# A two-layer hybrid decoder trunk on one core: low-rank products, merged steps, GpSimd's norm work and the expert stage's gathers rearranged

## The chip, the cores and the metric

The kernel runs on one core of one Trainium2 chip. The metric is the device time of one execution in microseconds (us). The kernel before takes 1657.32 us (median of three runs, 1655.43 to 1660.0). In the text TensorE is the matrix engine (PE in the rows, its weight loads PEld), VectorE is DVE, ScalarE is ACT, GpSimd is POOL, and SyncE (SP) issues the DMA transfers. Every instruction queue works in its own program order, and engines wait for each other by semaphores.

## The reference

256 tokens of width 1024 go through two layers. Each layer is a mixer and an expert stage, each followed by a layer norm of `ALPHA * h + result`:

```python
for l in range(DEPTH):                                   # 2
    z = h @ w_in[l]                                      # gates, conv, RWKV-7, attention
    y_a = (conv_b * causal_depthwise_conv(conv_c * conv_h, conv_w)) @ p_a
    y_b = rwkv7_time_mix(...) @ p_b                      # decay = f(tanh(xw) @ w2), a = sigmoid(a0 + xa @ a2)
    y_c = dilated_attention_branch(z_attn, cos, sin) @ p_c
    mix = (gate_a * y_a + gate_b * y_b + gate_c * y_c) @ w_o
    h = layer_norm(ALPHA * h + mix, ln1_g[l], ln1_b[l])
    # group-limited top-2 of 16 experts, SwiGLU
    for e in range(16):
        hid = silu(h @ w_gate[e]) * (h @ w_up[e])        # 1024 -> 512
        ffn += combine[..., e:e + 1] * (hid @ w_down[e]) # 512 -> 1024
    h = layer_norm(ALPHA * h + ffn, ln2_g[l], ln2_b[l])
```

All of it is float32.

## The kernel before, in words

**Dense products.** A float32 operand is split into a rounded high part and the rounded remainder (`hilo`: ScalarE casts, VectorE or GpSimd subtracts), and a product is three matmuls (`mm3`, lines 400 to 402). Names ending in h and l are such parts (wh, wl of a weight tile, xh, xl of the tokens), `dw` and `dt` are the dense products' PSUM banks. A matmul of rounded parts (fp32r) is one pass; one of plain float32 is two passes, and the trace has a record for each. Weight tiles of 512 KB are loaded ahead (`AHEAD` = 5 tiles) and split ahead (`SPLIT` = 2).

**Mixer.** A written table (`STAGES`) sets the order of the dense stages: waves (four per layer: r, k, v of four RWKV heads each), convolutions, attention heads, gates and output products. What belongs to a stage beside the dense product is a chain, a generator (`lows`, `wave`, `attention`). After every four steps of a dense product `pump` lets each live chain go on to its next `yield`; TensorE's queue thus holds dense matmuls with short groups of a chain's matmuls between them. The groups that matter here: in `wave` the low-rank products `pw` (decay) and `pa` (a), lines 490 to 495, whose high parts have 128 rows and whose remainder products 64, and the products `zb` (line 616, four pairs on alternating row halves, with a `yield` after two of them); in `attention` the scores `sc` (line 893, with a `yield` between two pairs of heads).

**Norm of the mixer's input.** The tokens that feed the dense products are transposed and split first (`xc`, `xh`, `xl`). The gain and offset for the residual copy of h (`ng`, `nb`) are loaded, GpSimd multiplies and adds (lines 1078, 1079: four operations of 128x1024), and SyncE stores the result to `hsave` (line 1080), from where it is read back at the mixer's end. This stands ahead of the first wave.

**Expert stage.** Tokens are ranked per expert, 64 places for each. Experts go in pairs p = 0 to 7, with shared work for each two pairs (even p). `places` (line 1303) makes the 0/1 matrix O of a group of four experts on VectorE. `gather` (line 1336) makes their tokens xg by matmul with O: in plain float32 from h, or, once `us` is set (at p = 4), from its rounded parts uh and ul. `gu` are the gate and up products (line 1389), `ht` the transposed hidden rows, `db` the down products (line 1440), `back` (line 1371) adds the weighted rows with the transposed O (`OT`) to the accumulators `acc`. `rows` (lines 1354 to 1364) makes OT by four transposes and the places' weights cs by four matmuls with two columns. At p = 7 the residual is added by float32 matmuls with ALPHA times the identity (line 1427), after GpSimd has applied gain and offset to h at p = 6. The expert weights (192 loads of 512 KB per layer, tiles `raw` and `mo`) are float32 and go straight into matmuls. After the last pair all engines read a count and may branch to an overflow path, which is not taken here.

Of the kernel before, what the change touches and what calls it, by code (L numbers as in the profile page):

```python
# [20 lines left out]
NE = 16  # L21
# [18 lines left out]
def _constants():  # L40
# [22 lines left out]
    out["alpha"] = ALPHA * np.eye(128)  # L63
# [163 lines left out]
class Net:  # L227
# [238 lines left out]
    def wave(self, l, w, r, k, v, lo, low, vf, yb):  # L466
# [21 lines left out]
        ps = self.bank("pw")  # L488
        for j in range(2):
            nc.tensor.matmul(ps[:, j * 256:j * 256 + 256], lh[:, 0, j * 128:j * 128 + 128], xh[:, 0, :], start=True, stop=False)  # L490
            nc.tensor.matmul(ps[:, j * 256:j * 256 + 256], lh[0:64, 0, j * 128:j * 128 + 128], xl[0:64], start=False, stop=True)
        pa = self.bank("pa")
        for j in range(2):
            nc.tensor.matmul(pa[:, j * 256:j * 256 + 256], lh[:, 1, j * 128:j * 128 + 128], xh[:, 1, :], start=True, stop=False)
            nc.tensor.matmul(pa[:, j * 256:j * 256 + 256], lh[64:128, 1, j * 128:j * 128 + 128], xl[64:128], start=False, stop=True)
# [365 lines left out]
    def attention(self, l, hh, g, q, k, v, st, yc):  # L861
# [24 lines left out]
        for qb in range(2):  # L886
# [3 lines left out]
            for hp in range(2):  # L890
# [3 lines left out]
                if hp == 0:  # L894
                    yield
# [98 lines left out]
    def mixer(self, l, h, vf):  # L994
# [238 lines left out]
    def moe(self, l, u, r, nm, lg):  # L1233
# [90 lines left out]
        V.tensor_copy(cnti, cnt)  # L1324
        over = s16("over")
# [20 lines left out]
        def rows(O, p):  # L1346

            b = self.bank("ot")
            ot = self.tg([128, 2, 256], "OT", F32R)
            cb = self.bank("cs")  # L1350
            for pp in range(2):
                for i in range(2):
                    o = O[:, i, 2 * pp:2 * pp + 2, :].rearrange("p e t -> p (e t)").bitcast(F32)
                    nc.tensor.transpose(b[:, pp * 256 + i * 128:pp * 256 + i * 128 + 128], o, self.c("ident"))
                for i in range(2):
                    o = O[:, i, 2 * pp:2 * pp + 2, :].rearrange("p e t -> p (e t)").bitcast(F32)
                    e = 2 * p + 2 * pp
                    nc.tensor.matmul(cb[:, 2 * pp:2 * pp + 2], o, comb[:, i, e:e + 2], start=(i == 0), stop=(i == 1))  # L1358
            V.tensor_copy(ot.rearrange("p a b -> p (a b)"), b)
            cs = self.sm([128, 2], "cs")  # L1360
            cv = cb[:, 0:4].rearrange("p (a e) -> p a e", e=2)
# [3 lines left out]
            return ot, cs  # L1365
# [13 lines left out]
        for p in range(NE // 2):  # L1379
            gu = []  # L1380
            for what in range(2):
                b = self.bank("gu")
                for k in range(KC):
                    if k % 2 == 0:
                        raw = [self.next_raw() for _ in range(2)]
                        if p == 0 and what == 0 and k + AH < KC:
                            gather(nxt, xg, k + AH)
                    for e in range(2):
# [3 lines left out]
                if what == 0:  # L1392
                    if late is not None:
                        back(*late)
                    if p % 2 == 0:
                        ot, cs = rows(nxt, p)
                        if p + 2 < NE // 2:
                            nxt, xn = places(p // 2 + 1), self.pair([128, 4, 2, 128], "xg")
                    if p == 4:

                        us = (self.pair([128, D], "uh", F32R), self.pair([128, D], "ul", F32R))
# [196 lines left out]
```

## Time and profile before

| | |
|---|---|
| median of three runs | 1657.32 us |
| profiled execution, its span | 1654.77 us, 1653.0 us |
| TensorE busy, mean granted clock | 1598.7 us (97%), 0.989 |
| VectorE, ScalarE, GpSimd busy | 956.6, 688.8, 75.8 us |
| moved by DMA | 370.02 MB, mean 224 GB/s |

A timeline row gives the start in us from the start of the span, the duration, engine, line, operation, names (written <- read), shape and count; a row with a count stands for that many instructions from its start on. In brackets is the idle time before it and who ended it. Matmul durations overlap, so the time that one takes in a stream is read from one start to the next. A layer of the mixer takes some 560 us, the expert stage some 235: layer 0 is mixer to 576 and expert stage from 586 to 822, layer 1 starts its dense work at 836.

### The profile page before, as it was taken

To read this page: it belongs to the slowest core of one execution; us is meant where nothing else is said; L and a number is where in the kernel's file an instruction comes from. 1 tells how busy PE (TensorE), PEld (TensorE's weight loads), DVE (VectorE), ACT (ScalarE), POOL (GpSimd) and SP (SyncE) were. 2 spreads that over 40 slices of the span, in tenths; PEclk is the share of its full clock that TensorE was granted. 3 is DMA by queue.
4 is the path that set the end of the run, shared out by engine and by line. 5 is a ranking of instruction groups with operands and counts; after the bars stand their busy time and mean duration, and the time that the engine had idled before them with its cause. 6 is when DMAs were issued, how large, how long until landed. Compare 5 with 4: busy or idle time off the path is not lost. (4 is left out here: it accounts for less than half of the span.)

```text
span 1653.0 us, 38103 instructions
## 1 busy us (share of the span) xinstructions
PE 1598.7 (97%) x16296; PEld 1254.0 (76%) x16296; DVE 956.6 (58%) x1768; ACT 688.8 (42%) x1236; POOL 75.8 (5%) x96
## 2 busy tenths in 40 slices
PE   6999999999999999999989999999999999999996
PEld 6999998988999954433379998899889999444332
DVE  6777767968765631121278678778687656211213
ACT  4554766757443311111145456666765433101110
POOL 4000000000000000002120000000000000000020
PEclk9999999999999999999989999999999999999998
DMA  8544443333458979999744434434334489799992
GB/s 308 174 133 153 136 140 97 129 116 100 141 169 304 355 294 405 409 409 383 274 167 138 147 123 129 132 122 129 120 109 155 154 333 359 290 410 410 409 402 86
DMA packets 102704, 370.02 MB, mean 224 GB/s; under 512 B 11392, under 2 KB 12416, under 8 KB 102528
## 3 DMA queue, kind: packets, MB, share of 16 engines
q1 hardware_dynamic: 102528, 367.51, 61.3%
q8 instruction: 130, 2.13, 0.5%
q14 instruction: 46, 0.38, 0.1%
HBM read 363.27 MB, written 4.19 MB: 222 GB/s over the span
## 5 line engine op out<-in xcount | busy, mean ns | idle before, releaser
L400 PE MATMUL dw<-xh,wh 128*128 128x256 f32 (+1 forms) x1584 | 472.6, 299 | 3.3 <-ACT wh L324 2.3
L401 PE MATMUL dw<-xl,wh 128*128 128x256 f32 (+1 forms) x1584 | 450.2, 284 | 5.7 <-DVE xl L325 5.7
L402 PE MATMUL dw<-xh,wl 128*128 128x256 f32 (+1 forms) x1584 | 449.6, 284 | 2.1 <-DVE wl L325 2.1
L325 DVE TENSOR_TENSOR wl<-raw,wh 128x1024 fp32r<-128x1024 f32 x272 | 329.6, 1224 | 55.3 <-ACT wh L324 24.6
L400 PEld LDWEIGHTS dw<-xh,wh 128*128 128x128 f32 (+1 forms) x1584 | 302.1, 191 | 25.1 <-issue 8.2
L324 ACT CAST wh<-raw 128x1024 fp32r<-128x1024 f32 x278 | 284.1, 1044 | 67.5 <-DVE wl L325 44.7
L401 PEld LDWEIGHTS dw<-xl,wh 128*128 128x128 f32 (+1 forms) x1584 | 303.2, 191 | 8.4 <-DVE xl L325 7.4
L402 PEld LDWEIGHTS dw<-xh,wl 128*128 128x128 f32 (+1 forms) x1584 | 302.9, 191 | 3.1 <-DVE wl L325 2.8
L1389 PE MATMUL gu<-raw,xg 128*64 128x512 f32 x592 | 139.0, 599 | 1.9 <-PE cs L1358 1.9
L1445 DVE SCALAR_TENSOR_TENSOR yl<-db,cs,yh 128x512 fp32r<-128x512 f32 x32 | 24.0, 751 | 148.0 <-ACT yh L1444 148.0
L1389 PEld LDWEIGHTS gu<-raw,xg 128*64 128x64 f32 x592 | 45.2, 137 | 81.1 <-issue 74.7
L1389 PE MATMUL gu<-mo,xg 128*64 128x512 f32 x432 | 104.0, 599 | 0.0
L1440 PE MATMUL db<-raw,hT 128*64 128x512 f32 x352 | 82.4, 596 | 1.3 <-ACT hT L1421 1.3
L1389 PEld LDWEIGHTS gu<-mo,xg 128*64 128x64 f32 x432 | 31.6, 138 | 55.5 <-issue 55.2
L1444 ACT ACTIVATE yh<-db,cs 128x512 fp32r<-128x512 f32 x32 | 22.0, 688 | 116.7 <-PE db L1440 116.7
L1410 ACT ACTIVATE th<-gu 128x512 f32<-128x512 f32 x16 | 9.6, 598 | 136.8 <-PE gu L1389 136.8
L1421 ACT COPY hT<-ht 128x512 f32<-128x512 f32 x16 | 9.4, 586 | 136.4 <-PE ht L1419 136.4
L1440 PEld LDWEIGHTS db<-raw,hT 128*64 128x64 f32 x352 | 25.1, 137 | 50.9 <-issue 47.9
L1412 DVE TENSOR_TENSOR th<-th,gu 128x512 f32<-128x512 f32 x16 | 11.0, 688 | 87.8 <-PE gu L1389 87.8
L400 PE MATMUL dt<-wh,xh 128*128 128x256 f32 x192 | 57.9, 302 | 0.0
L1411 DVE SCALAR_TENSOR_TENSOR th<-th,gu 128x512 f32<-128x512 f32 x16 | 11.0, 688 | 80.5 <-ACT th L1410 80.4
L401 PE MATMUL dt<-wl,xh 128*128 128x256 f32 x192 | 54.7, 285 | 0.0
(368 smaller groups left out, 2858.9 us busy)
## 6 DMA issues: line engine op xcount, KB each, us to landing
raw<-in_wm SPq DMA_DIRECT2D x272, 512.0 KB, 3.6
raw<-in_we SPq DMA_DIRECT2D x236, 512.0 KB, 10.2
mo<-in_we SPq DMA_DIRECT2D x148, 512.0 KB, 10.2
lo<-in_lo SPq DMA_DIRECT2D x8, 512.0 KB, 3.6
ng<-in_norms SPq DMA_DIRECT2D x5, 512.0 KB, 10.2
nb<-in_norms SPq DMA_DIRECT2D x5, 512.0 KB, 10.2
raw<-in_wl SPq DMA_DIRECT2D x4, 512.0 KB, 8.4
hsave<-h SPq DMA_DIRECT2D x4, 512.0 KB, 2.8
```

The costliest lines, as they stand in the source:

```text
L324: r = self.nc.scalar.copy(hi, src)
L325: (eng or self.nc.vector).tensor_tensor(lo, src, hi.bitcast(F32), op=ALU.subtract)
L400: nc.tensor.matmul(out, lh, rh, start=first, stop=False)
L401: nc.tensor.matmul(out, lh, rl, start=False, stop=False)
L402: nc.tensor.matmul(out, ll, rh, start=False, stop=last)
L1389: nc.tensor.matmul(b[64 * e:64 * e + 64, :], xg[k // 4][:, k % 4, p % 2, 64 * e:64 * e + 64], raw[e][:, k % 2, :], start=(k == 0), stop=(k ...
L1410: nc.scalar.activation(t, gu[0], AF.Tanh, scale=0.5)
L1411: V.scalar_tensor_tensor(t, t, 1.0, gu[0], op0=ALU.add, op1=ALU.mult)
L1412: V.tensor_tensor(t, t, gu[1], op=ALU.mult)
L1440: nc.tensor.matmul(b[64 * e:64 * e + 64, :], ht[:, k, 64 * e:64 * e + 64], raw[e][:, k % 2, :], start=(k == 0), stop=(k == 3))
L1444: last = nc.scalar.activation(yh, b, AF.Copy, scale=w)
L1445: V.scalar_tensor_tensor(yl, b, w, yh.bitcast(F32), op0=ALU.mult, op1=ALU.subtract)
```

## The change

Nine edits. In `wave` the four 128-row matmuls of `pw` and `pa` stand first, then the four 64-row ones, changing between the two row halves and banks. The `yield` inside the `zb` groups and the one inside the `sc` groups are gone. GpSimd's four operations and hsave are written after the first stage of the mixer (n == 1). In the expert stage a constant tile `pick` holds the identity and both halves' combine weights in rounded parts; `rows` uses two matmuls of 160 columns per spot (transposed O and weights in one), in two spots: after the first product and in the middle of the second, and the next `places` follows the second spot. The split into uh and ul is made at p = 0 after its own gathers, on ScalarE and VectorE. The residual is written to the same uh and ul, scaled by ALPHA and split again at p = 7, and added with the identity in rounded parts. The constant `alpha` is gone.

```diff
@@ wave
-        for j in range(2):
-            nc.tensor.matmul(ps[...], lh[:, 0, ...], xh[:, 0, :], start=True, stop=False)
-            nc.tensor.matmul(ps[...], lh[0:64, 0, ...], xl[0:64], start=False, stop=True)
-        pa = self.bank("pa")
-        for j in range(2):
-            nc.tensor.matmul(pa[...], lh[:, 1, ...], xh[:, 1, :], start=True, stop=False)
-            nc.tensor.matmul(pa[...], lh[64:128, 1, ...], xl[64:128], start=False, stop=True)
+        for n, b in enumerate((ps, pa)):
+            for j in range(2):
+                nc.tensor.matmul(b[...], lh[:, n, ...], xh[:, n, :], start=(j == 0), stop=False, ...)
+        for j in range(2):
+            for n, b in enumerate((ps, pa)):
+                o = slice(64 * n, 64 * n + 64)
+                nc.tensor.matmul(b[...], lh[o, n, ...], xl[o], start=False, stop=True, ...)
@@ wave, zb
-                if c == 1:
-                    yield
@@ attention, sc
-                if hp == 0:
-                    yield
@@ mixer
-        g, b = self.norm_params(2 * l)
-        for i in range(2):
-            nc.gpsimd.tensor_tensor(h[i], h[i], g, op=ALU.mult)
-            nc.gpsimd.tensor_tensor(h[i], h[i], b, op=ALU.add)
-            nc.sync.dma_start(self.hsave[l, i], h[i])
...
         for n, (what, j) in enumerate(STAGES[l]):
+            if n == 1:
+                g, b = self.norm_params(2 * l)
+                for i in range(2):
+                    nc.gpsimd.tensor_tensor(h[i], h[i], g, op=ALU.mult)
+                    nc.gpsimd.tensor_tensor(h[i], h[i], b, op=ALU.add)
+                    nc.sync.dma_start(self.hsave[l, i], h[i])
@@ expert stage
+        for i in range(2):
+            wh, wl = (pick[...] for j in range(2))
+            self.hilo(wh, wl, comb[:, i, :])
-        def rows(O, p):
+        def rows(O, p, pp, ot, cs):
+            n = 2 * NE
             b = self.bank("ot")
-                    nc.tensor.transpose(b[...], o, self.c("ident"))
...
-                    nc.tensor.matmul(cb[:, 2 * pp:2 * pp + 2], o, comb[:, i, e:e + 2], start=(i == 0), stop=(i == 1))
-            V.tensor_copy(ot.rearrange("p a b -> p (a b)"), b)
+            for i in range(2):
+                o = O[:, i, 2 * pp:2 * pp + 2, :].rearrange("p e t -> p (e t)")
+                nc.tensor.matmul(b[:, 128 * i:128 * i + 128 + n], o, pick[:, n * (1 - i):n * (1 - i) + 128 + n], start=(i == 0), stop=(i == 1), ...)
+            V.tensor_copy(ot[:, pp, :]..., b[...])
             for e in range(2):
-                V.tensor_copy(cs[h], cv[h, :, e])
+                V.tensor_reduce(cs[h, pp:pp + 1], w, axis=AX.X, op=ALU.add)
...
                         if p == 0 and what == 0 and k + AH < KC:
                             gather(nxt, xg, k + AH)
+                        elif p == 0 and what == 0 and us is None:
+                            us = (self.pair([128, D], "uh", F32R), self.pair([128, D], "ul", F32R))
+                            for i in range(2):
+                                self.hilo(us[0][i], us[1][i], u[i])
+                    if what and k == 4 and p % 2 == 0:
+                        rows(nxt, p, 1, ot, cs)
+                        if p + 2 < NE // 2:
+                            nxt, xn = places(p // 2 + 1), self.pair([128, 4, 2, 128], "xg")
...
-                    if p == 4:
-                        us = (...)
-                        for i in range(2):
-                            self.hilo(us[0][i], us[1][i], u[i], nc.gpsimd if i else V)
+                        ot, cs = self.tg([128, 2, 256], "OT", F32R), self.sm([128, 2], "cs")
+                        rows(nxt, p, 0, ot, cs)
...
+            if p == NE // 2 - 1:
+                for i in range(2):
+                    nc.scalar.activation(us[0][i], u[i], AF.Copy, scale=ALPHA)
+                    V.scalar_tensor_tensor(us[1][i], u[i], ALPHA, us[0][i].bitcast(F32), op0=ALU.mult, op1=ALU.subtract)
...
             if p == NE // 2 - 1:
-                for hf in range(2):
-                    for i in range(2):
-                        nc.tensor.matmul(acc[i][hf], self.c("alpha"), u[i][...], start=False, stop=False)
+                for part in us:
+                    for hf in range(2):
+                        for i in range(2):
+                            nc.tensor.matmul(acc[i][hf], pick[:, 2 * NE:2 * NE + 128], part[i][...], start=False, stop=False)
```

TensorE's queue at the low-rank block of the first wave of layer 0, before (xrh is the high part, xs the remainder, lh the low-rank weights; the row's last entry is the output):

```order
L402 MATMUL dw_530<-xh_149,wl_467 128x256
L490 MATMUL pw_568<-xrh_283,lh_549 128x256
L491 MATMUL pw_568<-xs_285,lh_549 128x256
L490 MATMUL pw_568<-xrh_283,lh_549 128x256
L491 MATMUL pw_568<-xs_285,lh_549 128x256
L494 MATMUL pa_573<-xrh_283,lh_549 128x256
L495 MATMUL pa_573<-xs_285,lh_549 128x256
L494 MATMUL pa_573<-xrh_283,lh_549 128x256
L495 MATMUL pa_573<-xs_285,lh_549 128x256
L400 MATMUL dw_530<-xh_148,wh_496 128x256
```

and at the same place in the changed kernel:

```order
L401 MATMUL dw_532<-xh_151,wl_459 128x256
L492 MATMUL pw_570<-xrh_285,lh_551 128x256 x2
L492 MATMUL pa_571<-xrh_285,lh_551 128x256 x2
L497 MATMUL pw_570<-xs_287,lh_551 128x256
L497 MATMUL pa_571<-xs_287,lh_551 128x256
L497 MATMUL pw_570<-xs_287,lh_551 128x256
L497 MATMUL pa_571<-xs_287,lh_551 128x256
L399 MATMUL dw_532<-xh_150,wh_488 128x256
```

The eight matmuls are the same; the change between 128 and 64 rows comes once inside the block, where it came seven times.

SyncE's queue around hsave at the start of layer 0, before (raw tiles from in_wm are the mixer's dense weights, lo the first wave's low-rank weights):

```order
L1075 DMA cstm_104<-in_cstm 128x1856
L295 DMA ng_287<-in_norms 128x1024
L296 DMA nb_288<-in_norms 128x1024
L1085 DMA lo_303<-in_lo 128x1024
L345 DMA raw_306<-in_wm 128x1024
L1080 DMA hsave<-h_114 128x1024
L1080 DMA hsave<-h_115 128x1024
L345 DMA raw_350<-in_wm 128x1024
L345 DMA raw_393<-in_wm 128x1024
```

and in the changed kernel:

```order
L1078 DMA lo_295<-in_lo 128x1024
L344 DMA raw_298<-in_wm 128x1024
L344 DMA raw_342<-in_wm 128x1024
L344 DMA raw_385<-in_wm 128x1024
L344 DMA raw_420<-in_wm 128x1024
L344 DMA raw_456<-in_wm 128x1024
L344 DMA raw_486<-in_wm 128x1024
L294 DMA ng_522<-in_norms 128x1024
L295 DMA nb_523<-in_norms 128x1024
L344 DMA raw_533<-in_wm 128x1024
L344 DMA raw_580<-in_wm 128x1024
L1159 DMA hsave<-h_116 128x1024
```

Eight weight loads stand ahead of hsave behind cstm, where one stood; ng and nb stand behind six of them.

TensorE's queue in the expert stage of layer 0 at the end of the first product of p = 0, before:

```order
L1389 MATMUL gu_8128<-mo_7629,xg_8113 64x512
L1354 MATMUL ot_8175<-ident,O_8088 128x128 x2
L1358 MATMUL cs_8177<-comb_8091,O_8088 128x2 x2
L1354 MATMUL ot_8175<-ident,O_8088 128x128 x2
L1358 MATMUL cs_8177<-comb_8091,O_8088 128x2 x2
L1389 MATMUL gu_8195<-mo_7674,xg_8112 64x512
```

and in the changed kernel, to the middle of the second product:

```order
L1358 MATMUL ot_8191<-pick,O_8090 128x160 x2
L1396 MATMUL gu_8197<-mo_7676,xg_8118 64x512
L1396 MATMUL gu_8197<-mo_7706,xg_8118 64x512
L1396 MATMUL gu_8197<-mo_7676,xg_8118 64x512
L1396 MATMUL gu_8197<-mo_7706,xg_8118 64x512
L1396 MATMUL gu_8197<-mo_7738,xg_8118 64x512
L1396 MATMUL gu_8197<-mo_7779,xg_8118 64x512
L1396 MATMUL gu_8197<-mo_7738,xg_8118 64x512
L1396 MATMUL gu_8197<-mo_7779,xg_8118 64x512
L1358 MATMUL ot_8218<-pick,O_8090 128x160 x2
```

Eight matmuls in one place became two and two, half a product apart.

## Rows read from the trace of the kernel before

**Rows 1.** Windows: stretch, length, busy by engine, clock, DMA share, GB/s.

```profile
33.00:40.00 7.00, 3.49 (x23) 3.08 (x22) 5.98 (x13) 5.08 (x10) 1.58 (x5) 0.91 0.86 289
60.00:576.00 516.00, 515.60 (x6743) 479.67 (x6743) 378.69 (x686) 281.80 (x511) 6.81 (x26) 1.00 0.49 163
660.00:822.00 162.00, 156.16 (x720) 63.93 (x716) 27.57 (x45) 23.01 (x37) 12.90 (x8) 1.00 0.95 374
837.00:849.00 12.00, 7.67 (x39) 6.78 (x40) 11.54 (x7) 2.70 (x4) 8.72 (x4) 0.72 0.31 111
```

**Rows 2.** Timeline of TensorE at a low-rank block; columns as described above.

```profile
53.63 0.28 PE L402 MATMUL dw<-xh,wl 128*128 128x256 f32 x1
53.75 0.28 PE L490 MATMUL pw<-xrh,lh 128*128 128x256 f32 x1
...
56.15 0.39 PE L400 MATMUL dw<-xh,wh 128*128 128x256 f32 x1
```

**Rows 3.** Timeline of TensorE at a zb group.

```profile
71.98 0.28 PE L402 MATMUL dw<-xh,wl 128*128 128x256 f32 x1
72.19 0.71 PE L616 MATMUL zb<-ar,bk 64*128 64x128 f32 x8
72.84 0.39 PE L400 MATMUL dw<-xh,wh 128*128 128x256 f32 x1
```

**Rows 4.** Timeline of TensorE at an attention's score group.

```profile
213.14 0.49 PE L893 MATMUL sc<-k,q 64*128 64x128 f32 x4
213.56 0.39 PE L400 MATMUL dw<-xh,wh 128*128 128x256 f32 x1
```

**Rows 5.** Timeline of SyncE, start of layer 0.

```profile
30.84 2.75 SPq L1080 DMA_DIRECT2D hsave<-h  x2
```

**Rows 6.** Timeline of VectorE, start of layer 1.

```profile
835.72 7.76 DVE L325 TENSOR_TENSOR xl<-xc,xh 128x512 fp32r<-128x512 f32 x3
...
846.73 0.68 DVE L325 TENSOR_TENSOR xl<-xc,xh 128x512 fp32r<-128x512 f32 x1
```

**Rows 7.** Timeline of GpSimd between the layers.

```profile
820.88 5.87 POOL L325 TENSOR_TENSOR wl<-raw,wh 128x1024 fp32r<-128x1024 f32 x3 [15.64 <-ACT wh L324]
```

**Rows 8.** Timeline of VectorE between the layers.

```profile
823.30 2.26 DVE L284 TENSOR_SCALAR lny<-v 128x2 int32<-128x2 int32 x1
```

**Rows 9.** Timeline of TensorE at two gathers, float32 and rounded parts.

```profile
668.54 1.99 PE L1336 MATMUL g<-O,h 128*128 128x256 f32 x8
670.37 0.60 PE L1419 MATMUL ht<-ident,th 128*128 128x128 f32 x4
...
755.54 0.48 PE L1336 MATMUL g<-O,uh 128*128 128x256 f32 x2
...
756.66 2.37 PE L1440 MATMUL db<-mo,hT 128*64 128x512 f32 x10
```

**Rows 10.** Timeline of TensorE at two blocks of places.

```profile
653.47 0.60 PE L1354 MATMUL ot<-ident,O 128*128 128x128 f32 x4
...
656.37 2.58 PE L1389 MATMUL gu<-raw,xg 128*64 128x512 f32 x5 [0.47 <-PE cs L1358]
...
772.62 0.39 PE L1371 MATMUL acc<-yl,OT 128*128 128x512 f32 x1
772.85 0.38 PE L1354 MATMUL ot<-ident,O 128*128 128x128 f32 x2
...
774.12 1.08 PE L1389 MATMUL gu<-raw,xg 128*64 128x512 f32 x4
```

**Rows 11.** Timeline of TensorE at p = 4.

```profile
728.86 0.39 PE L1336 MATMUL g<-O,ul 128*128 128x256 f32 x1 [1.20 <-DVE ul L325]
```

**Rows 12.** Timeline of TensorE at the residual.

```profile
808.07 2.74 PE L1427 MATMUL acc<-h,cst 128*128 128x512 f32 x6
```

**Rows 13.** Timeline of SyncE, last expert loads.

```profile
780.09 7.86 SPq L345 DMA_DIRECT2D raw<-in_we  x7
```

**Rows 14.** The page, part 6: DMA issues, KB each, us to landing.

```profile
raw<-in_we SPq DMA_DIRECT2D x236, 512.0 KB, 10.2
```

More of the change, by code (lines that the diff above doesn't have):

```diff
@@ L62, in _constants @@
     out["ones"] = np.ones((128, 128))
-    out["alpha"] = ALPHA * np.eye(128)
     am = []
@@ L1324, in moe @@
         V.tensor_copy(cnti, cnt)
+        pick = self.pick
+        for i in range(2):
+            wh, wl = (pick[:, (1 - i) * (128 + 2 * NE) + NE * j:(1 - i) * (128 + 2 * NE) + NE * j + NE] for j in range(2))
+            self.hilo(wh, wl, comb[:, i, :])
         over = s16("over")
@@ L1344, in gather @@
                     nc.scalar.activation(d, b[:, 0:256], AF.Identity, bias=bi, scale=sc)
-        def rows(O, p):
+        def rows(O, p, pp, ot, cs):
+            n = 2 * NE
             b = self.bank("ot")
-            ot = self.tg([128, 2, 256], "OT", F32R)
-            cb = self.bank("cs")
-            for pp in range(2):
-                for i in range(2):
-                    o = O[:, i, 2 * pp:2 * pp + 2, :].rearrange("p e t -> p (e t)").bitcast(F32)
-                    nc.tensor.transpose(b[:, pp * 256 + i * 128:pp * 256 + i * 128 + 128], o, self.c("ident"))
-                for i in range(2):
-                    o = O[:, i, 2 * pp:2 * pp + 2, :].rearrange("p e t -> p (e t)").bitcast(F32)
-                    e = 2 * p + 2 * pp
-                    nc.tensor.matmul(cb[:, 2 * pp:2 * pp + 2], o, comb[:, i, e:e + 2], start=(i == 0), stop=(i == 1))
-            V.tensor_copy(ot.rearrange("p a b -> p (a b)"), b)
-            cs = self.sm([128, 2], "cs")
-            cv = cb[:, 0:4].rearrange("p (a e) -> p a e", e=2)
+            for i in range(2):
+                o = O[:, i, 2 * pp:2 * pp + 2, :].rearrange("p e t -> p (e t)")
+                nc.tensor.matmul(b[:, 128 * i:128 * i + 128 + n], o, pick[:, n * (1 - i):n * (1 - i) + 128 + n], start=(i == 0), stop=(i == 1), skip_group_check=True)
+            V.tensor_copy(ot[:, pp, :].rearrange("p (a t) -> p a t", a=2), b[:, 0:256 + 2 * n].rearrange("p (a t) -> p a t", a=2)[:, :, 0:128])
             for e in range(2):
                 h = slice(64 * e, 64 * e + 64)
-                V.tensor_copy(cs[h], cv[h, :, e])
-            return ot, cs
+                w = b[h, 128:128 + n].rearrange("p (a e) -> p e a", a=2)[:, 2 * p + 2 * pp + e, :]
+                V.tensor_reduce(cs[h, pp:pp + 1], w, axis=AX.X, op=ALU.add)
         def back(p, hf, ot, yy):
@@ L1424, in moe @@
             if p == NE // 2 - 1:
-                for hf in range(2):
-                    for i in range(2):
-                        nc.tensor.matmul(acc[i][hf], self.c("alpha"), u[i][:, hf * 512:hf * 512 + 512], start=False, stop=False)
+                for part in us:
+                    for hf in range(2):
+                        for i in range(2):
+                            nc.tensor.matmul(acc[i][hf], pick[:, 2 * NE:2 * NE + 128], part[i][:, hf * 512:hf * 512 + 512], start=False, stop=False)
             if p == NE // 2 - 3:
@@ L1549, in build @@
                             self.plan.append((ap["we"][l, 2 * p + e, w], 2, False))
+            self.pick = self.const.tile([128, 128 + 4 * NE], F32R, name="pick")
+            nc.scalar.copy(self.pick[:, 2 * NE:2 * NE + 128], self.ident)
             self.dv = self.const.tile([128, DEPTH * NDV], F32, name="dv")
```

13 lines of the change are left out of this document (4 added, 9 removed).

## The prediction

> **What bounds the kernel now.** I read busy time by stretches first. In the token mixer of layer 0 TensorE is busy 515.6 of 516 us, in the expert stage 156 of 162 us, while VectorE has a quarter of the mixer free [rows 1]. So TensorE sets the pace nearly everywhere, and an edit is worth what it takes from TensorE's own row of work. The exceptions are two short stretches at the starts of the layers, where TensorE is idle for a third to a half [rows 1], and the norm between the layers. The second thing to see is the DMA share of 0.95 in the expert stage [rows 1]: there transfers are a bound close behind TensorE. Everything below is taken from TensorE's timeline (start to next start, since matmuls overlap), then from the queues that move.
>
> **The low-rank block.** A dense matmul follows the last one after 0.12 us (53.63 to 53.75), and the eight matmuls of the block, alternating between 128 and 64 rows, take from 53.75 to 56.15: 2.40 us, 0.3 from each to the next [rows 2]. Now four of 128 rows stand in a row, then four of 64 rows that change between the upper and the lower half and between two banks. The first four should follow each other as dense ones do, 3 x 0.12, then one change at 0.21 (as 71.98 to 72.19 [rows 3]), three steps of 0.06 to 0.12 and one change back: 0.36 + 0.21 + 0.27 + 0.21 = 1.05. The 0.06 is what the small f32 matmuls on alternating halves show: eight in 0.65 us (72.19 to 72.84), less the change of 0.21 at their end, 0.44 / 7 [rows 3]. Saved: 2.40 - 1.05 = 1.35, taken as 1.4 with the dense neighbours, in 8 blocks (4 waves in 2 layers): 11. If the price of 0.30 stays with the 64-row ones, 0.7 x 8 = 5.6; if the pairs overlap wholly, 12.
> The Trainium skill, "TensorE: Matmul & The Clock Gate", Part 3, The mechanism, says that a weight load overlaps a running matmul only when the row group differs, which speaks against four 128-row matmuls behind each other. The dense rows, each with new 128-row weights 0.12 us apart, don't agree with it. By the rule the four would keep 0.30 each, a block would save 1.4 - 4 x 0.18 = 0.7, and the sum would be 5.5 us worse.
>
> **Merged steps.** A group of eight small matmuls between dense ones costs 72.84 - 71.98 - 0.12 = 0.74 [rows 3], and about 0.1 more on the dense matmul after it. Two groups cost 1.68; one of sixteen 0.84 + 8 x 0.06 = 1.32. Saved 0.36, in 16 places: 5.8. A group of the attention's four score matmuls costs 213.56 - 213.14 + 0.2 = 0.6, of which four times 0.07 = 0.3 is its own matmuls ((0.42 - 0.21) / 3 from one to the next) [rows 4]; 24 places would save up to 0.3 each, but often another chain's work stands next to the group and there is no change to save. I take half: 3.6 (0 to 7). VectorE reads the banks only when both groups are done, before and now, so no wait is added. Mixer together: 11 + 5.8 + 3.6 = 20.4.
>
> **The four GpSimd operations and hsave behind the first wave.** In layer 0 SyncE holds the weight loads behind hsave until 30.84 [rows 5], and in 33 to 40 TensorE is busy 3.49 of 7 us at a granted clock of 0.91 [rows 1]: 3.5 + 0.6 = 4.1 lost. In layer 1 VectorE needs 7.76 us for three xl that take 0.68 when alone [rows 6], while GpSimd works through the whole stretch; TensorE is idle 4.3 of 12 us with a mean clock of 0.72 [rows 1], the lower level for about half of it; on the 7.67 busy us that is 0.28 x 7.67 = 2.1, together 6.4. One us of it stays, since VectorE's own work in that stretch is as long as TensorE's. Gain 4.1 + 5.4 = 9.5. It comes back in part: the operations now stand beside the first wave, and hsave stays ahead of weight loads in SyncE's queue, with seven loads moved ahead of it. Five tiles ahead and two or more split ones cover 7 x 24 x 0.12 = 20 us, GpSimd needs 10. So I take 2 us per layer (0 to 6). Net 5.5.
> The Trainium skill, "SBUF — State Buffer", SBUF: two separate sides, calls the pair of ports that VectorE and GpSimd share an exclusive lock, held for a whole instruction. The three xl at 2.6 us each agree; by it the 10 us move, and are not gone, which is the third rival.
> At the seam between the layers the high parts on ScalarE and the low parts on GpSimd, started at 820.88 [rows 7], now stand behind the branch. VectorE's tiny steps of the norm are held up by GpSimd there (2.26 us for a step on 128x2) [rows 8], and a later GpSimd holds them up longer: 0 to 2.3, taken 1.5 lost.
>
> **The expert stage, per layer.** Gathers: eight in f32 take 668.54 to 670.37 = 1.83, eight in rounded parts 755.54 to 756.66 = 1.12 [rows 9]. As the split is made at p = 0, two more groups of four calls go from one to the other: 8 x 0.71 = 5.7.
> Places: of four blocks two take 653.47 to 656.37 = 2.90, with a wait for VectorE inside, two 772.85 to 774.12 = 1.27 [rows 10]: 8.3. Now two spots per block, each two matmuls of 160 columns with no wait between. No row has this form. Bounds: 0.35 a spot if they run as dense ones (two at 0.12 and a change), 0.9 if each costs two passes as f32 does. I take 0.45, since the nearest rows are rounded ones: 8 x 0.45 = 3.6, saved 4.7 (1.1 to 5.5). VectorE's comparison for the next places now starts half a product later, with the other half until the gather that needs it. If that cover is too short, the wait that such work causes now, 2.90 - 1.27 = 1.6, comes back in up to three blocks.
> Split: the wait of 1.20 at p = 4 [rows 11] goes. At p = 0 the whole second product covers VectorE's two low parts. Taken 1.2.
> Residual: eight passes of 0.43 (six in 2.74) [rows 12] become eight of 0.23 (772.62 to 772.85) [rows 10]: 1.6. The two scaled copies and two subtractions stand at p = 7 where VectorE and ScalarE wait for the products; nothing lost.
> Sum 5.7 + 4.7 + 1.2 + 1.6 = 13.2, in two layers 26.4. Are the weights there in time? The last seven loads of the layer are issued by 787.95 [rows 13] and land 10.2 us after issue [rows 14], at 798. The last products, which use them, follow the residual that ends near 810.8 [rows 12] and fill the stretch behind it. So 13 to 20 us of lead are left at the end, and TensorE takes 13 of them. The holding of four more buffers for the split rows from p = 0 on takes up to four loads (7.86 / 7 = 1.1 us each), 4.5 us. It is just enough.
>
> **Sum.** 20.4 + 5.5 - 1.5 + 26.4 = 50.8 us. The profiled execution took 1654.8 (span 1653.0 and 1.8 around it): 1604.0. The median of the runs shown is 2.5 above that execution, so I forecast 1606.
>
> **Rivals.**
> First, the transfers take over in the expert stage. For it: the DMA share of 0.95, and a lead that shrinks while TensorE gains. Against it: the lead above. If buffers come free too late by 6 to 7 us per layer, half of the 26 is lost: 1619.
> Second, the new forms don't run as their neighbours do: the block keeps 0.30 for half of its matmuls (6 lost), the 160-column matmuls take two passes (7), the merged scores give nothing (4): 1623. For it: no row has just these forms. Against it: 0.06 on alternating halves, 0.12 in the dense stream.
> Third, the port conflict only moves: beside the first wave VectorE loses the same 7 us, its low parts come late and the clock falls as in 837 to 849. Then the net 5.5 and some 4 more are gone: 1615. Against it: tiles are split ahead there, which they were not at the layer's start.
> Fourth, slower: SyncE stands behind hsave for as long as GpSimd needs, and GpSimd now works where VectorE is busy 73% of the time [rows 1]. If GpSimd gets its port only in VectorE's gaps, its 10 us stretch; beyond the 20 us of tiles in hand each further us is TensorE's, in both layers. From a stretch of 46 us on (2 x 26 lost, about the sum) the kernel is slower than before; at 55 us 2 x 35 = 70 are lost: 1676. Against it: at 837 to 849 it was VectorE that was stretched, GpSimd hardly (8.72 busy for its own work).
>
> **How the numbers follow.** My forecast has 0.58, with its own range 1593 to 1617; the first rival 0.15, the second 0.12, the third 0.10, the fourth 0.04; 0.01 is for none. Better than forecast it gets by full overlap and all merged scores, 1590. For 8 times in 10 I take 1588 to 1628. A measurement of this kernel tells 0.3%, 5 us, from no change. All cases but the fourth are faster by more; leaving some room for several at once, 0.94 faster, 0.02 within, 0.04 slower.
>
> **What would show it.** In the profile after: the low-rank block from 2.4 to about 1.1 us; fewer entries into the dense stream with groups of sixteen; no idle TensorE at 33 to 40 and clock near 1.0 there and at the start of layer 1; hsave later, with weight loads ahead of it; eight-matmul gathers of 1.1 us from p = 1 on; spots of 0.35 to 0.9 us for the places, without a wait for VectorE; the expert stage some 13 us shorter in each layer. It would be wrong if TensorE waits for in_we landings late in the expert stage, for in_wm behind hsave, or for low parts beside the first wave.

## The result, and the profile after

The changed kernel takes 1629.5 us (median of four, 1625.8 to 1630.5), the kernel before 1658.1 beside it: ratio 0.9825, interval 0.9804 to 0.9846. That is 28.6 us faster, where 50.8 were worked out; the time lies just above the range given. The profiled execution has a span of 1628.0, 25.0 less.

To see where it went I cut both traces at the same work: the mixer from its first to its last dense matmul, the expert stage from its first gather to its last acc matmul, the seam from there to the next layer's first dense matmul (start to start, us):

| | before | after | gained | forecast |
|---|---|---|---|---|
| mixer, layers 0 and 1 | 558.7, 561.1 | 551.4, 555.1 | 13.3 | 25.9 |
| expert stage, layers 0 and 1 | 234.6, 232.9 | 227.2, 227.9 | 12.4 | 26.4 |
| seam | 15.4 | 15.3 | 0.1 | -1.5 |

About half is missing in both stages. One trace tells such a sum to some 4 us: two other runs below have the changed kernel's mixers unaltered, and these took 548.2 and 555.3, and 551.3 and 556.1. And 1.7 of the 7.4 gained in the expert stage of layer 0 is a stretch in the trace before (655 to 661, granted clock 0.72) that layer 1 doesn't have. The page after, part 1 (busy us, share, count):

```profile
PE 1562.9 (96%) x16232; PEld 1237.1 (76%) x16232; DVE 966.5 (59%) x1802; ACT 694.1 (43%) x1245; POOL 72.7 (4%) x94
```

TensorE's share fell from 97 to 96%: part of what was taken from its work came back as idle time. By stretch (columns as in [rows 1]):

```profile
40.00:60.00 20.00, 17.38 (x130) 16.76 (x129) 17.32 (x19) 8.89 (x16) 8.36 (x7) 0.91 0.42 141
60.00:549.00 489.00, 484.63 (x6557) 456.24 (x6556) 365.81 (x668) 278.52 (x508) 6.78 (x26) 1.00 0.47 156
...
850.00:1377.00 527.00, 519.27 (x6824) 489.44 (x6824) 394.45 (x707) 291.02 (x532) 9.03 (x31) 0.99 0.50 165
```

The mixer of layer 0, where TensorE was idle 0.4 of 516 us [rows 1], now has 4.4 idle in 489, and that of layer 1 has 7.7 in 527. The low-rank block and a merged zb group on TensorE's timeline, which answer to [rows 2, 3]:

```profile
170.25 0.28 PE L401 MATMUL dw<-xh,wl 128*128 128x256 f32 x1
170.37 0.41 PE L492 MATMUL pw<-xrh,lh 128*128 128x256 f32 x2
170.61 0.40 PE L492 MATMUL pa<-xrh,lh 128*128 128x256 f32 x2
170.94 0.38 PE L497 MATMUL pw<-xs,lh 64*128 64x256 f32 x1
170.94 0.38 PE L497 MATMUL pa<-xs,lh 64*128 64x256 f32 x1
...
171.37 0.39 PE L399 MATMUL dw<-xh,wh 128*128 128x256 f32 x1
```

```profile
70.56 0.28 PE L401 MATMUL dw<-xh,wl 128*128 128x256 f32 x1
70.77 1.16 PE L618 MATMUL zb<-ar,bk 64*128 64x128 f32 x16
71.86 0.39 PE L399 MATMUL dw<-xh,wh 128*128 128x256 f32 x1
```

Both are as worked out: the block takes 170.37 to 171.37 = 1.00 (forecast 1.05, before 2.40), and sixteen matmuls cost 71.86 - 70.56 - 0.12 + 0.1 = 1.28 (forecast 1.32). So the prices were right. What was not forecast stands in the brackets. TensorE's timeline at three places (idle time before the row, and who ended it):

```profile
51.87 0.50 PE L492 MATMUL pw<-xrh,lh 128*128 128x256 f32 x2 [2.62 <-DVE lh L478]
...
86.90 0.74 PE L677 MATMUL mw<-TT,XE 32*32 32x32 f32 x64 [2.32 <-DVE TT L685]
...
848.72 0.39 PE L401 MATMUL dw<-xh,wl 128*128 128x256 f32 x1 [2.50 <-DVE wl L324]
```

The first and the third stand behind GpSimd's moved operations, which on its timeline run at 36 to 47 and, with durations alike, at 840 to 851, as soon as ng has landed (here layer 0):

```profile
36.37 4.94 POOL L1157 TENSOR_TENSOR h<-h,ng 128x1024 f32<-128x1024 f32 x2 [15.29 <-DMA ng<-in_norms]
41.27 5.92 POOL L1158 TENSOR_TENSOR h<-h,nb 128x1024 f32<-128x1024 f32 x2
```

Beside them two steps xs on VectorE take 3.05 us (0.85 where GpSimd starts only behind most of them, see below), and a wl takes 3.31, against 1.22 alone:

```profile
34.86 1.22 DVE L324 TENSOR_TENSOR wl<-raw,wh 128x1024 fp32r<-128x1024 f32 x1
35.99 3.05 DVE L1063 TENSOR_TENSOR xs<-xr,xrh 64x256 fp32r<-64x256 f32 x2
...
41.62 3.31 DVE L324 TENSOR_TENSOR wl<-raw,wh 128x1024 fp32r<-128x1024 f32 x1
```

The second wait, for TT, is of another kind: GpSimd is idle there. TT is the last of a row of VectorE steps that begins with the results of zb, on VectorE's timeline:

```profile
76.68 1.28 DVE L620 TENSOR_TENSOR Z<-zb,cstm 128x512 f32<-128x512 f32 x2
...
85.18 1.22 DVE L324 TENSOR_TENSOR wl<-raw,wh 128x1024 fp32r<-128x1024 f32 x1
86.31 0.44 DVE L685 STREAM_TRANSPOSE TT<-TT 128x256 f32<-128x256 f32 x1
```

From 76.68 to 86.75 VectorE works nearly without a gap, part of it at the dense products' own wl. TensorE comes to its next step before that row is through. Behind this wait the clock falls to the lower of its two levels (1.2 GHz), from 87.9 to 91.3, and the same happens behind a wait of 2.27 for TT at 987.5:

```profile
86.00:92.00 6.00, 5.10 (x146) 4.81 (x147) 5.82 (x11) 4.16 (x5) 0.00 (x0) 0.72 0.37 132
986.00:994.00 8.00, 6.55 (x157) 6.27 (x158) 6.74 (x11) 4.07 (x7) 0.00 (x0) 0.79 0.36 100
```

In the expert stage, TensorE's timeline at the first and the second spot of the places at p = 2:

```profile
646.87 0.35 PE L1358 MATMUL ot<-pick,O 128*128 128x160 f32 x2
648.01 1.51 PE L1396 MATMUL gu<-raw,xg 128*64 128x512 f32 x6 [0.80 <-PE ot L1358]
...
655.05 0.45 PE L1358 MATMUL ot<-pick,O 128*128 128x160 f32 x2
655.43 1.08 PE L1396 MATMUL gu<-raw,xg 128*64 128x512 f32 x4
```

The second spot takes 0.38, the first 1.14: the second product waits there. The same at p = 4 and 6. At the end of p = 0:

```profile
603.57 0.39 PE L1341 MATMUL g<-O,uh 128*128 128x256 f32 x1 [1.17 <-ACT uh L323]
...
605.07 3.65 PE L1447 MATMUL db<-raw,hT 128*64 128x512 f32 x14 [0.56 <-ACT hT L1427]
```

Waits for hT, which ScalarE copies from the transposed hidden rows, come at other places too, in the list of TensorE's waits of this expert stage (us in total, times, longest):

```profile
PE g L1341 <- ACT hT L1427: 1.3, 2, 0.7
PE db L1447 <- ACT hT L1427: 1.2, 2, 0.7
```

Before, one of 0.7 us stood there. Set side by side in layer 1, start to start and without waits: the gathers take 20.8 instead of 26.8 us, the places 3.0 instead of 5.9 (their waits 2.4 instead of 2.5), the residual 2.2 instead of 3.6. But the wait for ul (1.20, [rows 11]) has become one for uh (1.17), the waits for hT grew by 1.9, the down products take 58.4 instead of 56.4 and the gate and up products 113.7 instead of 112.5.

No TensorE wait for a landing of in_we is in the trace.

### The profile page after: what moved, and what is told of

It reads as the page before. It is cut to its first block, busy times and chain, and to the rows that moved or that the text cites. A ratio compares the mean times of both kernels' runs of the same rounds, so it can differ in the third digit from the quotient of the medians.

```text
span 1628.0 us, 37966 instructions
## 1 busy us (share of the span) xinstructions
PE 1562.9 (96%) x16232; PEld 1237.1 (76%) x16232; DVE 966.5 (59%) x1802; ACT 694.1 (43%) x1245; POOL 72.7 (4%) x94
## 5 line engine op out<-in xcount | busy, mean ns | idle before, releaser
L324 DVE TENSOR_TENSOR wl<-raw,wh 128x1024 fp32r<-128x1024 f32 x272 | 337.2, 1248 | 57.1 <-ACT wh L323 27.0
L1447 PE MATMUL db<-raw,hT 128*64 128x512 f32 x352 | 86.6, 597 | 2.5 <-ACT hT L1427 2.5
L400 PE MATMUL dt<-wl,xh 128*128 128x256 f32 x192 | 54.7, 285 | 0.0
L401 PE MATMUL dt<-wh,xl 128*128 128x256 f32 x192 | 54.2, 282 | 0.0
L1359 DVE CAST OT<-ot 128x256 fp32r<-128x256 f32 x16 | 6.8, 425 | 68.9 <-PE ot L1358 68.9
## 6 DMA issues: line engine op xcount, KB each, us to landing
raw<-in_we SPq DMA_DIRECT2D x236, 512.0 KB, 10.2
mo<-in_we SPq DMA_DIRECT2D x148, 512.0 KB, 10.2
ng<-in_norms SPq DMA_DIRECT2D x5, 512.0 KB, 10.1
nb<-in_norms SPq DMA_DIRECT2D x5, 512.0 KB, 10.1
```

Source lines behind the costliest of these rows:

```text
L324: (eng or self.nc.vector).tensor_tensor(lo, src, hi.bitcast(F32), op=ALU.subtract)
L400: nc.tensor.matmul(out, lh, rl, start=False, stop=False)
L401: nc.tensor.matmul(out, ll, rh, start=False, stop=last)
L1359: V.tensor_copy(ot[:, pp, :].rearrange("p (a t) -> p a t", a=2), b[:, 0:256 + 2 * n].rearrange("p (a t) -> p a t", a=2)[:, :, 0:128])
L1447: nc.tensor.matmul(b[64 * e:64 * e + 64, :], ht[:, k, 64 * e:64 * e + 64], raw[e][:, k % 2, :], start=(k == 0), stop=(k == 3))
```

## The experiments

My theory from the trace: the steps taken out of the chains were time in which VectorE and ScalarE did their part (A); the port conflict of the GpSimd work only changed its place; and in the expert stage the 160-column form is fast, but a PSUM bank and a split that is not ready stop TensorE. The rivals stand with each run. Ratios are to the kernel before, run beside it; the changed kernel is at 0.9825.

**The yield in the zb groups back.**

```diff
                     nc.tensor.matmul(zb[q][:, o:o + 128], ...)
+                if c == 1:
+                    yield
```

> The changed kernel with the yield inside the zb groups put back, so 32 groups of eight matmuls instead of 16 of sixteen. Theory A (the merge took the time that VectorE needed between the groups and the first 32x32 product, which now waits 8.4 us in all for TT): these waits fall to about 1 us, 6.2 us of entries into the dense stream come back, total 1627 to 1632, no slower than the changed kernel. Theory B (the waits come from a VectorE that is late for another reason, GpSimd's port or the merged scores): the waits stay near 8 us and the time rises by 6, to about 1635.

Ratio 0.9841 (0.9824 to 0.9857). The mixers took 554.5 and 551.8: 3.1 more in layer 0, 3.3 less in layer 1. The waits for TT fell from 8.4 to about 2.5, but others came in their place (0.8 to 1.5 us each at sb, nb and bb, for VectorE and ScalarE). So A held for TT, and taken over both layers the zb merge was worth nothing that these two traces can tell; but the waits don't belong to one of the merges alone.

**An empty step for each zb group.**

```diff
                                         zb[q].rearrange(...), zm, op=ALU.mult)
             yield
+            yield
```

> The changed kernel with the zb groups merged but one more empty yield after each merged group, so that the wave has as many steps as before. Theory A (the steps were time for VectorE): the waits of the 32x32 products for TT go as in the kernel before while the 6.2 us of entries stay saved: 1621 to 1625. Theory B (VectorE is late for another reason): waits stay near 8 us, 1628 to 1631.

Ratio 0.9822 (0.9805 to 0.9838): less than expected by A. The waits for TT are 4.2, and again there are new ones at sb (0.8, 0.8, 1.5) and bb (1.1). The wave has its old length, the attention has not, and they now meet at other places.

**Both yields back, and both as empty steps.** The first undoes both merges; the second keeps the groups merged and gives every chain as many steps as before.

```diff
 # both back: the two "if ...: yield" of the kernel before
 # both as empty steps:
                     nc.tensor.matmul(b[e][...], qT[...], kT[...], start=True, stop=True)
             yield
+            yield
 ...
                                         zb[q].rearrange(...), zm, op=ALU.mult)
             yield
+            yield
```

> The changed kernel with both yields back, in the zb and in the sc groups; the rest of the change stays. Theory A (together the merges are worth nothing: the steps taken out were time for VectorE and ScalarE, and what the entries save comes back as waits in all chains): waits in the mixers fall from some 20 us to those of before plus the ones of the move, the time is 0 to 3 us under the changed kernel (ratio to before 0.981 to 0.983). Theory B (the merges are worth their forecast 9.4): the ratio rises to 0.987 or above.

> The changed kernel with both groups merged, and each yield that was taken out put behind the merged group as an empty step, so that every chain has as many steps as before. Theory A (it is the number of steps that VectorE and ScalarE need): few waits as without merges, the entries stay saved: 6 to 9 us under the kernel without merges, ratio 0.976 to 0.978. Theory B (the waits hang on the place of the groups against each other, not on the number of steps): the ratio is 0.981 to 0.985.

Ratios 0.9828 (0.9811 to 0.9844) and 0.9741 (0.9725 to 0.9758). Without any merge the kernel is as fast as the changed one, so the two merges together were worth nothing; the mixers took 553.3 and 551.3, 1.9 less than after. With the empty steps they took 545.6 and 547.4: 13.5 less than after, 11.6 less than without merges. Theory A gets more than it asked for. Windows of TensorE's stretches in the version with both empty steps:

```profile
60.00:549.00 489.00, 487.33 (x6605) 459.65 (x6604) 374.82 (x677) 281.15 (x508) 6.82 (x26) 1.00 0.48 161
850.00:1365.00 515.00, 513.01 (x6817) 485.26 (x6816) 390.71 (x703) 290.13 (x531) 7.99 (x30) 1.00 0.50 169
```

TensorE is idle 1.7 and 2.0 us there, against 4.4 and 7.7 (in 850 to 1365) after; without merges it is 1.6 and 2.3. Both mixers together, from first to last dense matmul, split by what TensorE does in them (an entry is a place where a dense matmul is followed by a chain's; its time goes from the start of that dense matmul to the start of the next dense one, idle time left out):

| | both yields back | changed kernel | both as empty steps |
|---|---|---|---|
| entries (before: 307) | 307 | 302 | 279 |
| time in them, us | 299.2 | 289.1 | 282.5 |
| idle, us | 10.2 | 18.5 | 12.1 |
| dense steps at the lower clock | 17 in 3.5 us | 57 in 12.0 us | 43 in 9.2 us |
| the other dense steps, us | 791.6 | 786.8 | 789.2 |

So the merges did take 10.1 us from TensorE's row, about the 9.4 forecast, though forty yields less made only 5 entries less: after the change the wave's and the attention's groups no longer came at the same places of the dense stream, and groups that had shared an entry stood alone (the wave's mw without a neighbour at 38 places, before at 28). What took the gain back is 8.3 us of idle time and the lower clock: a dense step takes some 0.21 us there instead of 0.125, so 40 more of them cost some 3.5 us. With the empty steps most of the idle time goes, and the groups meet as before: 23 entries less than after, 6.6 us less in them.

**GpSimd's operations back ahead of the first wave, and written one per stage.**

```diff
 # back:   the block ahead of the first wave, as in the kernel before
 # spread, in the loop over the stages:
-                for i in range(2):
-                    nc.gpsimd.tensor_tensor(h[i], h[i], g, op=ALU.mult)
-                    nc.gpsimd.tensor_tensor(h[i], h[i], b, op=ALU.add)
-                    nc.sync.dma_start(self.hsave[l, i], h[i])
+            if 1 <= n < 5:
+                i, add = (n - 1) // 2, (n - 1) % 2
+                nc.gpsimd.tensor_tensor(h[i], h[i], hb if add else hg, op=ALU.add if add else ALU.mult)
+                if add:
+                    nc.sync.dma_start(self.hsave[l, i], h[i])
```

> The changed kernel with GpSimd's four operations and hsave ahead of the first wave again. Theory A (the move only carried the port conflict to another place: TensorE waits 2.6 us for lh at 51.9 with the clock at 0.91 in 40 to 60, and 2.5 us for wl at 848.7): the stalls of before at 33 to 40 and 837 to 849 return, some 4 and 6 us, the new ones of 4.5 and 3 go: 1630 to 1634, that is 1 to 4 slower than the changed kernel. Theory B (the move is worth its forecast 5.5 us or more): 1635 or above.

> The changed kernel with GpSimd's four operations one at each of the stages 1 to 4 instead of all four at stage 1. Theory A (four operations of 2.5 us in a row hold VectorE up for longer than the tiles split ahead cover): the waits at 51.9 and 848.7 and the lower clock behind the first go, 1621 to 1625. Theory B (any operation of GpSimd costs TensorE what it takes, wherever it stands): the same waits in pieces, 1628 to 1631.

Ratios 0.9868 (0.9848 to 0.9887) and 0.9838 (0.9822 to 0.9855). Back: 7.1 us slower than the changed kernel by the ratios; the mixers took 549.4 and 560.9, that is 3.9 more than after, and 2.9 and 6.8 more than in the two runs below that leave the mixers as they are. In layer 1 the old place is 4.8 to 5.8 worse in all three comparisons. In layer 0 no difference is shown: 549.4 lies between the 548.2 and 551.4 of the same changed mixer. At the place itself the move shows: the 400th dense matmul of the layer starts 62.6 us (layer 0) and 65.9 (layer 1) behind its first with the old place, 61.8 and 59.9 after, 59.8 and 60.2, and 61.8 and 61.2 in the other two. That is 5.5 to 8.5 gained in the two layers together. The totals don't decide between A and B: 1634.1 is at the end of A's range, 7.1 by the ratios is B's.

The second run is no test of its theories. The operations were written at four stages, but on GpSimd's timeline they ran in a row as in the changed kernel, once ng had landed (in layer 1 from 837.0 to 847.8):

```profile
35.33 5.17 POOL L1157 TENSOR_TENSOR h<-h,ng 128x1024 f32<-128x1024 f32 x2 [15.41 <-DMA ng<-in_norms]
40.47 6.75 POOL L1157 TENSOR_TENSOR h<-h,nb 128x1024 f32<-128x1024 f32 x2
```

The mixers took 548.4 and 556.4, the wait for lh was 0.71 instead of 2.62 us, the one for wl in layer 1 still 2.62. The shorter wait for lh is not the edit's: with the operations at stage 1, in the run with the first spot ahead, it was 0.70. There GpSimd started at 35.46, when VectorE's two steps xs were nearly done, and did not hold them up:

```profile
34.77 0.85 DVE L1063 TENSOR_TENSOR xs<-xr,xrh 64x256 fp32r<-64x256 f32 x2
```

**The first spot ahead of the late acc matmuls.**

```diff
-                    if late is not None:
-                        back(*late)
+                    was = late
                     if p % 2 == 0:
                         ...
                         rows(nxt, p, 0, ot, cs)
+                    if was is not None:
+                        back(*was)
```

> The changed kernel with the first spot of the places ahead of the four late acc matmuls instead of behind them. Theory A (the second product's bank is the one that the places just left, so it waits 0.8 us for VectorE's cast, in three spots of each layer): with four matmuls of 0.23 between, the wait goes, 4.6 us in all, ratio about 0.9798. Theory B (the 160-column form itself is slow, or what follows it waits for something else): 0.9825 as the changed kernel.

Ratio 0.9809 (0.9791 to 0.9826); the expert stages took 224.5 each, 2.7 and 3.4 less than after (2.6 by the ratios, whose intervals overlap). The wait is gone, on TensorE's timeline at p = 2:

```profile
641.39 0.46 PE L1358 MATMUL ot<-pick,O 128*128 128x160 f32 x2
641.68 0.43 PE L1369 MATMUL acc<-yh,OT 128*128 128x512 f32 x1
...
642.74 3.65 PE L1396 MATMUL gu<-raw,xg 128*64 128x512 f32 x16
```

In the built program of the changed kernel the second product's accumulator stands in the very PSUM bank that the places were written to just before, at p = 2, 4 and 6 (not at p = 0, where the spot takes 0.38 too). So its first matmul had to wait until VectorE had read the bank out: at p = 2 VectorE's last read of it ends at 647.91, and the product starts at 648.01. The 160-column form itself is fast: 0.29 for two with the change.

**The split used from p = 1 on.**

```diff
-                            us = (self.pair(..., "uh", F32R), self.pair(..., "ul", F32R))
+                            parts = (self.pair(..., "uh", F32R), self.pair(..., "ul", F32R))
 ...
                 gather(nxt, xn, p % 2 * 4 + 2)
+                us = parts
```

> The changed kernel with the split made at the same place, but used from p = 1 on, so that the two gathers at the end of p = 0 are in float32 again. Theory A (at p = 0 TensorE waits for uh and hT, some 2.5 to 3 us per layer, because the split comes too late for the first gathers): the waits go, two gathers cost 0.75 more each, so 1 to 1.5 us per layer are gained, ratio 0.9805 to 0.9815. Theory B (the waits are there with float32 too): 1.5 us per layer are lost, 0.984 to 0.985.

Ratio 0.9802 (0.9786 to 0.9819); the expert stages took 225.4 each, 1.8 and 2.5 less (3.8 in all by the ratios). On TensorE's timeline the end of p = 0 has no wait, though its gathers are float32:

```profile
602.27 1.99 PE L1341 MATMUL g<-O,h 128*128 128x256 f32 x8
604.11 0.60 PE L1425 MATMUL ht<-ident,th 128*128 128x128 f32 x4
604.54 1.89 PE L1341 MATMUL g<-O,h 128*128 128x256 f32 x8
606.37 7.09 PE L1448 MATMUL db<-raw,hT 128*64 128x512 f32 x32
```

**The low-rank block alone.** The kernel before with only that edit:

```diff
+        for n, b in enumerate((ps, pa)):
+            for j in range(2):
+                nc.tensor.matmul(b[...], lh[:, n, ...], xh[:, n, :], start=(j == 0), stop=False, ...)
         for j in range(2):
-            nc.tensor.matmul(ps[...], lh[:, 0, ...], xh[:, 0, :], start=True, stop=False)
-            nc.tensor.matmul(ps[...], lh[0:64, 0, ...], xl[0:64], start=False, stop=True)
-        ...
+            for n, b in enumerate((ps, pa)):
+                o = slice(64 * n, 64 * n + 64)
+                nc.tensor.matmul(b[...], lh[o, n, ...], xl[o], start=False, stop=True, ...)
```

> The kernel before with the low-rank block of the change alone. Theory A (1.4 us per block, eight blocks, nothing behind it): ratio 0.9930 to 0.9935. Theory B (VectorE's and ScalarE's chains lose time here too, since the block is shorter): part of it comes back, 0.995 to 0.998.

Ratio 0.9917 (0.9900 to 0.9934); the mixers took 553.9 and 556.2, 9.7 less together than before, 13.7 by the ratio. (The profiled execution, 1645.5, was the longest of four with a median of 1643.3, so 9.7 is rather too little.) TensorE's time in the entries fell from 309.4 to 298.6, by 10.8. The block was worth about what it was priced at, without a wait behind it.

**All parts that gained.** Empty steps, first spot ahead, split from p = 1 (the diffs above), and in the first version GpSimd's operations written at four stages in layer 0:

```diff
+            for part in range(4):
+                if n == (1 + part if l == 0 else 1):
+                    i, add = part // 2, part % 2
+                    nc.gpsimd.tensor_tensor(h[i], h[i], hb if add else hg, op=ALU.add if add else ALU.mult)
+                    ...
```

> The kernel with both merged groups and the steps put back as empty ones, the places' first spot ahead of the late acc matmuls, the split used from p = 1 on, and in layer 0 GpSimd's operations one per stage. If the parts add: from 0.974 another 2.6 + 3.8 + 3 us, ratio 0.968 to 0.970. If the transfers of the expert weights take over once TensorE is that fast (the lead at the stage's end was worked out as 13 to 20 us, less what is gained), the expert stage stays near 227 us and the ratio is 0.972 to 0.975, with TensorE waiting for in_we landings.

> As the version with all parts, but with GpSimd's four operations at stage 1 in both layers as in the changed kernel. If spreading them in layer 0 is worth its 3 us also here, this ratio is 0.0015 to 0.002 above that version's; if the wait for lh at 51 was hidden by something else, equal.

Ratios 0.9670 (0.9657 to 0.9683), 1601.5 us against 1656.2, and 0.9682 (0.9669 to 0.9696). That is 54.7 us, more than the 50.8 forecast for the change, and 25.7 better than the changed kernel, where the three parts alone make 20.3 by their ratios. The mixers took 542.6 and 544.9, in the second version 544.2 and 544.5, against 545.6 and 547.4 with the empty steps alone. The second version's mixers are the very same as those, so up to 4.3 of the surplus is what one trace differs from another. The expert stages took 222.6 each, and TensorE waits for no landing. Of the waits named above those for wl in layer 1 (2.8 at the longest), for TT (3.2 in all) and for lh (0.7) are left. Whether GpSimd's operations gain by being spread stays untested: in layer 0 they ran in a row in both versions, from 36.1 to 47.8 and from 35.4 to 47.3.

## Why the prediction was wrong

The direction was right, the size was not: 28.6 us instead of 50.8, and the range ended 1.5 us short.

- **Low-rank block: right.** 11 forecast; 1.00 instead of 2.40 per block in the trace, 10.8 in the entries with this edit alone. The Trainium skill's rule on weight loads ("TensorE: Matmul & The Clock Gate", Part 3, The mechanism: overlap only when the row group differs) is not borne out here: two matmuls of 128 rows start at 170.37 and the next two, with other weights, 0.24 later, though one such load takes 0.19 us. The same section also lets a load run ahead into a background weight buffer, and that these rows don't contradict.
- **Merged steps: the step that failed most.** The prediction said that "VectorE reads the banks only when both groups are done, before and now, so no wait is added", and counted 9.4. Its price for TensorE's own work was right (10.1 measured). The first half of the sentence is true of the banks and beside the point. A yield is not only an entry into the dense stream but four dense steps of time, in which VectorE, with 10 us of nearly unbroken work between zb and TT, gets on. Taking it out moved TensorE's next step ahead of VectorE's result: 8.3 us of idle time, and some 3.5 at the lower clock, part of it behind those waits. Net the merges were worth nothing (-1.9 in the mixers, 0.5 by the ratios). Shown by the runs with both yields and with both empty steps: merged with the time kept they are worth 11.6 in the mixers, 14.4 by the ratios.
- **GpSimd's move: not shown to be off.** Net 5.5 was forecast; the runs show 2.9 to 6.8 in the mixers and 7.1 by the ratios. What it gains at the layer's start comes back in part, as forecast: in layer 0 the 200th dense matmul comes 5.5 us sooner than with the old place, the 400th only 0.8 to 2.8. The cover of 20 us was counted for weight tiles; the first wait was for lh, the low-rank weights, which no tile ahead covers (0.70 to 2.66 us from run to run). The Trainium skill's lock on the shared port ("SBUF — State Buffer", SBUF: two separate sides) agrees: a wl of 3.31 us instead of 1.22 beside the operations at their new place.
- **Seam.** 1.5 lost was taken, 0.1 gained; it is 14.4 to 15.7 in all runs, so neither is shown.
- **Expert stage: gathers and residual right, places and split too good, two costs missing.** In layer 1: the gathers gained 5.9 (5.7 forecast), the residual 1.4 (1.6). The places were to take 0.45 per spot "with no wait between"; they take 0.38 where nothing waits and 1.14 in three spots per layer, because of the bank: 3.1 gained where 4.7 was forecast. At p = 0 "the whole second product covers VectorE's two low parts" failed: ScalarE's uh came 1.17 late, so the split gained nothing where 1.2 was forecast. Not in the sum at all were the waits for hT, 1.9 more, to which TensorE now comes sooner, and some 3 us more in the float32 products. Of the latter 1.15 at p = 0 goes when the gathers there are float32 again; that the rest too comes from rounded groups between float32 ones is an inference. Both edits together, in the version with all parts, give back 4.6 and 5.3 per layer of the 5.8 and 8.2 that were missing.
- **Rivals.** The transfers did not take over, even with the expert stage 10 to 12 us shorter: the lead was enough. The new forms ran as forecast. The third rival, that the conflict only moves, held in part: beside the operations wl and xs are late, but most of the gain stayed. The fourth did not come: hsave was issued 13 us later in layer 0, and TensorE and ScalarE waited for no in_wm tile behind it.
- The range was too narrow because each term was bounded by the price of its own work. The common cause, that less work on a full TensorE uncovers the engines beside it in several places at once, was left as single rivals, and the one for the mixer's chains was missing.

Left open: why the lower clock follows some of the waits of over 2 us and not others of the same length (in the trace after two of the three for TT, in the run with the first spot ahead one of the same three), and whether GpSimd's operations, really spread, would spare VectorE.

## What to carry to other kernels

In a queue that interleaves two kinds of work, the points where they change also give time to the engines beside it: when a group is merged to save an entry, put that time back as an empty step, and count the entries in the new order rather than the yields taken out. When an edit shortens what TensorE does next to another engine's result, look for the next wait of that kind in the order (a bank just left, a cast just issued) and put other ready work between. Moving work off a stall is worth what the stall costs less what it costs at the new place; a trace of that place shows both better than the total. And after such an edit look at the engine's own timeline: operations written at later stages still ran in a row here, once the gain that the first waits for had landed.

## What the runs showed of the hardware

- Two 64-row matmuls on opposite row halves and different banks start together (170.94 and 170.94), a pair each 0.22 us; alternating with 128-row ones each cost 0.30 [rows 2].
- Two rounded matmuls of 160 columns, with 128-row weights each, take 0.38 us between float32 ones, 0.29 ahead of rounded ones.
- A rounded matmul of 256 columns takes 0.12 us in a stream [rows 2]; one of plain float32 leaves two records of about 0.23 each (eight in 1.83 [rows 9]), so it takes about four times as long.
- After the wait of 2.62 us at 51.87 the clock falls to the lower of its two levels, 1.2 GHz: the stretch 40 to 60 has a granted clock of 0.91, and on TensorE's timeline the dense matmuls begin 0.11 apart, then 0.22. With a wait of 0.70 instead, in the run with the first spot ahead, the same stretch has 1.00:

```profile
53.41 0.28 PE L400 MATMUL dw<-xl,wh 128*128 128x256 f32 x1
53.52 0.28 PE L401 MATMUL dw<-xh,wl 128*128 128x256 f32 x1
...
53.77 0.42 PE L400 MATMUL dw<-xl,wh 128*128 128x256 f32 x1
53.99 0.42 PE L401 MATMUL dw<-xh,wl 128*128 128x256 f32 x1
```
